# Weight sums of pair 0 made ahead for six feed-forward groups, four of them by way of DRAM

## The chip, the cores and the metric

The kernel runs on one core of one Trainium2 chip. The metric is the device time of one execution in microseconds (us), the median of several runs. The engines are named as in the profile: PE (TensorE, the matmuls), PEld (TensorE's weight loads), DVE (VectorE), ACT (ScalarE), POOL (GpSimd) and SP (SyncE, which here does nothing but issue DMAs). "SPq" is SP's queue of issues.

## The reference

One block of a network in float32, for 256 tokens of width 2048: a projection into several branches, a gated delta rule and a sparse attention, two gates, an output projection, and a feed-forward part with D_FF = 5632. The change bears on the feed-forward part's first matrix:

```python
x = layer_norm(DEEPNORM_ALPHA * x + merged @ w_out[l], ln1_g[l], ln1_b[l])
h_gate, h_up = jnp.split(x @ w_ffn_in[l], 2, axis=-1)
x = layer_norm(DEEPNORM_ALPHA * x + (jax.nn.silu(h_gate) * h_up) @ w_ffn_out[l], ln2_g[l], ln2_b[l])
```

## The kernel before

**Numbers in two parts.** PE multiplies in a short float type (`F32R`). Each float32 operand v is therefore split into a high part `hi` (a cast, on ACT) and a low part `lo = v - hi` (a subtraction, on DVE), and each product takes three matmuls: hi x hi, hi x lo, lo x hi (`mm3`, L213 to L215).

**Chunks.** Weights arrive as chunks of 128 x 1024 (512 KB). `chunk` (its DMA is L85, its cast L87, its subtraction L89) loads one into `raw` on SP and makes `hi` and `lo`. `raw`, `hi` and `lo` have four buffers each, so a load waits for a `raw` that ACT and DVE have done with, and a cast waits for a `hi` that PE has done with.

**Groups and pairs.** After the first layer norm the feed-forward part's first matrix is worked off in 512 gate and 512 up columns at a time: a first one in two blocks (`wfi`), then ten groups i = 1 to 10 (`wfg[i - 1]`, the loop from L1388 to L1399). A group has eight pairs q = 0 to 7, each of two chunks, and sums all of them in PSUM, for two blocks of 128 tokens and two halves of 512 columns. `x_group` (L1031) runs the pairs in a given order. A pair is done in one of two ways:

- plain (`plain_pair`): two chunks, eight products, 24 matmuls;
- with seven products (`seven_pair`, L265), after Strassen's way of multiplying 2 x 2 blocks: 21 matmuls. It needs differences of the activations (`f_form`, made once by `x_form`) and four sums of weight blocks, t1 to t4 (`sum13` L242, `sum24` L246 and L247), each split again (`f_thi` by ACT L237, `f_tlo` by DVE L238). Its loads are L276 (`f_wraw`) and L278 (`raw`). Where the sums are there already (`ready`), it loads one chunk and a half and makes none of them.

`FQ` lists the pairs with seven products: 4 and 6 in group 1, and 2, 4 and 6 in the others. The seven-product sums gather in four further PSUM banks; after the last such pair `sums_chain` (L1018) adds them up on DVE and ACT. The groups swap the two sets of four banks.

**After a group** `hidden_chain` (L1347) makes silu(gate) x up, transposes it on PE, splits it into the tiles `hH`, `hL` (from group 3 on at index i - 3), and makes forms of it for the second matrix. `hH7` to `hH10` hold the buffers of `seven_pair` until then (`f_home`: two each of `wraw`, `wt`, `thi`, `tlo`).

**What sets the order.** PE and SP run in the order in which the program is written; DVE, ACT and POOL are ordered by a scheduler, by priority:

```python
ctx.enter_context(tc.manual_schedule(engines={mybir.EngineType.PE, mybir.EngineType.SP}))
```

Work beside the matmuls is written as generators ("chains"). `tick()` is called after each chunk, or twice in a seven-product pair, and moves every chain on whose time has come; `yield n` waits n ticks, `yield "name"` for an event. `f_forms_chain` (L1330) makes the forms while the second `wfi` block and group 1 run. A DMA in a chain on SP takes its place in SP's order at the tick at which it is written.

Of the kernel before, what the change touches and what calls it, by code (L numbers as in the profile page):

```python
# [8 lines left out]
F32 = mybir.dt.float32  # L9
F32R = mybir.dt.float32r  # L10
# [7 lines left out]
P = 128  # L18
# [14 lines left out]
LEAD = 70  # L33
# [10 lines left out]
ZO = (0, 1, 3, 2, 4, 5, 6, 7)  # L44
OQ = (0, 2, 4, 6)
WALL = sorted({*WQ[0], *WQ[1]})
FQ = ((4, 6), *[(2, 4, 6)] * 9)
OUT_AT = (8, 9, 10)

LN2_LOAD = (5, 7, 9, 11)  # L50
# [9 lines left out]
def block_kernel(ctx: ExitStack, tc: tile.TileContext, xT, x, cpack, onehot, relb, convw, alog, dtb, gnw,  # L60
                 ws, wws, win, wz, wgt, wba, wbb, woa, wob, wfi, wfg, wfo, ln1g, ln1b, ln2g, ln2b, out):
    nc = tc.nc
# [6 lines left out]
    dr = ctx.enter_context(tc.tile_pool(name="dr", bufs=1, space=DRAM))  # L69
# [10 lines left out]
    def chunk(src, pool=None, lead=LEAD):  # L80
        n = src.shape[1]
        pool = pool or wp
        with tc.high_priority(offset=lead):
            raw = wp.tile([P, n], F32, name="raw", tag="raw")
            nc.sync.dma_start(raw, src)  # L85
            hi = pool.tile([P, n], F32R, name="hi", tag="hi")
            nc.scalar.copy(hi, raw)  # L87
            lo = pool.tile([P, n], F32R, name="lo", tag="lo")
            nc.vector.tensor_sub(lo, raw, hi.bitcast(F32))  # L89
        return hi, lo  # L90
# [5 lines left out]
    def start(gen, at_once=False):  # L96
        chains.append([gen, clock[0] + (next(gen) if at_once else 0)])
# [17 lines left out]
    def event(name):  # L115
        done[name] = clock[0]
# [86 lines left out]
    def split(hi, lo, src):  # L203
        nc.scalar.copy(hi, src)
        nc.vector.tensor_sub(lo, src, hi.bitcast(F32))
# [99 lines left out]
    def forms(g, a1, a2, b1, b2):  # L305

        nc.vector.tensor_sub(g[0], a2, b2)
        nc.vector.tensor_sub(g[1], a1, g[0])
        nc.vector.tensor_sub(g[2], a2, a1)
        nc.vector.tensor_sub(g[3], b1, g[1])  # L310
# [26 lines left out]
    def T(name, shape, dtype=F32, tag=None):  # L337
        return p1.tile(shape, dtype, name=name, tag=tag or name)
# [62 lines left out]
    def need(*names):  # L401
        for n in names:
            assert n in done, n
# [27 lines left out]
    for i in range(8):  # L431
        k0 = 2 * i
        parts = [srcs[i]] if i > 2 else [srcs[i][:, :512], srcs[i][:, 512:]]
        for j, src in enumerate(parts):
            k, n = k0 + j, 2 // len(parts)
# [8 lines left out]
            else:  # L444
                split(*xp, xr)
                hi, lo = chunk(src, lead=0)
# [28 lines left out]
    def taps(y, src, c):  # L475
        nc.scalar.activation(y, src, AF.Copy, scale=cw[:, c, 3:4])
        for j in (1, 2, 3):
            nc.vector.scalar_tensor_tensor(y[:, j:], src[:, :S - j], cw[:, c, 3 - j:4 - j], y[:, j:],
                                           op0=OP.mult, op1=OP.add)

    def conv_first(dst, pss):
        for i in range(4):
            taps(dst[:, i, :], pss[i // 2][:, (i % 2) * S:(i % 2 + 1) * S], 8 + i)
        nc.scalar.activation(dst[:, 0:4], dst[:, 0:4], AF.Silu)
# [436 lines left out]
    for ch in (gates_chain, key_chain, query_chain, value_chain, index_chain, attend_chain, out_gate_chain):  # L921
        start(ch())

    conv_first(s_kT, pss)
    event("kc0")
    for dst, h0, c0, ev in ((s_kT, 4, 12, "kc1"), (s_qT, 0, 0, "qc0"), (s_qT, 4, 4, "qc1"),
# [18 lines left out]
    def halves(*tiles):  # L945
        return [0, [t[:, i] for t in tiles for i in range(2)]]

    def two(name, dtype, old):
        return T(name, [P, 2, 1024], dtype, tag=old)

    def z_chain():

        yield "v1"
        yield 1
        t0 = [rp.tile([P, 2, 1024], F32R, name=f"z_t{i}", tag=f"x1_{i}") for i in range(2)]
        wt = two("z_wt", F32, "ol_")
        gates_home.update(wraw=halves(two("z_wraw", F32, "oh_")), wt=halves(wt), thi=halves(t0[0]), tlo=halves(t0[1]))
        for q, old in ((4, "s_ak"), (6, "s_sq")):
            t = T(f"g_form{q}", [P, 2, 4, P], F32R, tag=old)
            gates_form[q] = t[:, 0], t[:, 1]  # L960
        gates_form[2] = [p1.tile([P, 4, P], F32R, name="g_form2", tag="rel", bufs=2) for _ in range(2)]
        yield from early_sums(wz, ZQ[0], home, z_ready)
        yield 1
        x_form(ZQ[0], gates_form[ZQ[0]], wt[:, 0, :512], wt[:, 0, 512:])
        yield "lg"
        t1 = two("z_t2", F32R, "s_vT"), two("z_t3", F32R, "s_t")
        for tag, *t in zip(("thi", "tlo"), t0, t1):
            gates_home[tag] = halves(*t)
            gates_home[tag][0] = 2
        yield from early_sums(wz, ZQ[1], home, z_ready)  # L970
        for q in ZQ[1:]:
            yield 1
            x_form(q, gates_form[q], wt[:, 0, :512], wt[:, 0, 512:])
        event("zready")
# [35 lines left out]
    def x_form(q, dst, x32, g):  # L1010
        x32 = x32.rearrange("p (k t) -> p k t", k=2)
        g = g.rearrange("p (i t) -> p i t", i=4)
        ks = slice(2 * q % 4, 2 * q % 4 + 2)
        nc.vector.tensor_add(x32, XH[q // 2][:, ks].bitcast(F32), XL[q // 2][:, ks].bitcast(F32))
        forms([g[:, j] for j in range(4)], x32[:, 0, :P], x32[:, 0, P:], x32[:, 1, :P], x32[:, 1, P:])
        split(*dst, g)

    def sums_chain(v, wbank):  # L1018

        p1_, n6, n7, n5 = wbank  # L1020
        with tc.high_priority(offset=LEAD):
            nc.scalar.copy(v[0], p1_)
            nc.scalar.copy(v[2], n6)
            nc.vector.tensor_sub(v[2], v[2], p1_)
            nc.vector.tensor_add(v[1], n5, v[2])
        yield 1
        with tc.high_priority(offset=LEAD):
            nc.vector.tensor_add(v[2], v[2], n7)
            nc.vector.tensor_add(v[3], n5, v[2])

    def x_group(src, sevens, std, shared, form_of, home, sums, at={}, order=range(KT // 2), ready={}):  # L1031

        bank = [std() for _ in range(4)]
        sevens = [q for q in order if q in sevens]
        for q in order:
            if q in at:
                at[q]()
            if q in sevens:
                if q == sevens[0]:
                    wbank = [shared() for _ in range(4)]  # L1040
                seven_pair(bank, wbank, src, xh, xl, q, lambda q: lambda f: [t[:, f] for t in form_of[q]], home,
                           q == sevens[0], q == sevens[-1], ready)
                if q == sevens[-1]:
                    start(sums(wbank))
            else:
                plain_pair(bank, src, xh, xl, q, q == order[0], q == order[-1])
        return bank
# [129 lines left out]
    def load_x(tb, g):  # L1177
        if not g:
# [4 lines left out]
    bank = x_group(woa, OQ, ps_acc, ps_aux, gates_form, home,  # L1183
                   lambda wbank: seven_chain(0, wbank, wo_room[:, 1024:1536]), {q: lambda tb=tb: load_x(tb, 0) for tb, q in enumerate(OO[6:])}, OO,
                   wo_ready)
# [7 lines left out]
    hp_ = fh.enter_context(tc.tile_pool(name="hp", bufs=1, side="left", reuse_waits="tile"))  # L1193
    hH, hL = [None] * (FT // 4), [None] * (FT // 4)

    def h_tile(pool, i):
        hH[i], hL[i] = (pool.tile([P, 4, S], F32R, name=f"{hl}{i}", tag=f"{hl}{i}") for hl in ("hH", "hL"))
# [13 lines left out]
        nc.sync.dma_start(t.rearrange("p k t -> p (k t)").bitcast(F32), d_h[i, j])  # L1211

    h_first = passing()
    for i in range(1, 5):
        h_tile(hp_, i)
    l1 = ExitStack()
    gp = l1.enter_context(tc.tile_pool(name="gp1", bufs=1, side="left", reuse_waits="tile"))
    ex = l1.enter_context(tc.tile_pool(name="ex1", bufs=4, side="left", reuse_waits="tile"))
# [71 lines left out]
    def fv():  # L1290
        return fp.tile([P, 512], F32, name="v", tag="v", bufs=4)
# [20 lines left out]
                  lambda tb, ps: start(h_chain(0, tb, gated(tb, ps), ps_aux)))  # L1312
    l1.close()
    hp2 = fh.enter_context(tc.tile_pool(name="hp2", bufs=1, side="left", reuse_waits="tile"))
    for i in (5, 6):
        h_tile(hp2, i)


    f_home = {}
    for tag, dtype, i in (("wraw", F32, 7), ("wt", F32, 8), ("thi", F32R, 9), ("tlo", F32R, 10)):  # L1320
        f_home[tag] = [0, [hp2.tile([P, 1024], dtype, name=f"f_{tag}", tag=f"{hl}{i}") for hl in ("hH", "hL")]]

    def fhome(tag):
        e = f_home[tag]
        e[0] += 1
        return e[1][e[0] % 2]

    f_form = {}

    def f_forms_chain():  # L1330
        yield "x1"
        for tb in range(NTB):
            yield 2
            nc.sync.dma_start(d_x1[tb], x1[tb])
        t = [rp.tile([P, 2, 2, 4, P], F32R, name="f_form", tag=f"x1_{tb}") for tb in range(NTB)]
        for i, q in enumerate((4, 2, 6)):
            yield 1
            f_form[q] = t[i // 2][:, i % 2, 0], t[i // 2][:, i % 2, 1]
            x_form(q, f_form[q], fv(), fv())

    start(f_forms_chain())
    for tb, ps in enumerate(block_xs([wfi[1, k] for k in range(8)], xh, xl)):
# [45 lines left out]
    for i in range(1, NG + 1):  # L1388
        std, shared = (ps_aux, ps_acc) if i % 2 else (ps_acc, ps_aux)
        sums = []  # L1390

        def places():
            sums.extend(fv() for _ in range(4))
            return sums

        bank = x_group(wfg[i - 1], FQ[i - 1], std, shared, f_form, fhome, lambda wbank: sums_chain(places(), wbank))
        if i == NG:
            h_tile(hp2, 7)
        start(hidden_chain(i, bank, sums, std), at_once=True)  # L1399
# [58 lines left out]
    bank = group(0, ps_aux, ps_acc, FT // 2)  # L1458
# [4 lines left out]
    bank = group(1, ps_acc, ps_aux, FT // 2 - HELD)  # L1463
# [194 lines left out]
```

## Time and profile before

| | us |
|---|---|
| median of 3 runs (1456.36 to 1457.3) | 1456.81 |
| the profiled execution's own time | 1456.99 |
| its span, from the first to the last instruction | 1455.2 |
| PE busy, of the span | 1447.2 |
| DVE busy | 1253.8 |
| ACT busy | 807.3 |
| POOL busy | 47.6 |
| loads and stores over the span | 314.89 MB, mean 216 GB/s |

Busy PE is the time in which any matmul is under way; matmuls overlap, so it says only that PE waited little. The granted clock of PE was 0.999 over the span. In the rows a line starts with the time or the source line, then the engine, the operation, what it writes <- what it reads, and the shape.

### The profile page before, as it was taken

What the parts mean: (1) busy time and instruction counts of PE and PEld (TensorE: products, weight loads), DVE (VectorE), ACT (ScalarE), POOL (GpSimd) and SP (SyncE); (2) the same over time, 40 slices, a digit from 0 to 9 for tenths busy, and PEclk for the clock granted to TensorE, in tenths of its full rate; (3) what the DMA queues carried; (4) which work ended last, traced back from release to release, by engine and by line L of the source; (5) the groups of instructions that cost most, each with busy time, mean ns of one, the idle gap of its engine ahead of it and who ended that gap; (6) DMA issues with size and microseconds to landing.
All of it is one profiled execution on the core that took longest, in us unless ns stands there. A gap on an engine that the chain in (4) does not pass through costs nothing.

```text
span 1455.2 us, 19528 instructions
## 1 busy us (share of the span) xinstructions
PE 1447.2 (99%) x7158; PEld 1217.6 (84%) x7158; DVE 1253.8 (86%) x1713; ACT 807.3 (55%) x1000; POOL 47.6 (3%) x59
## 2 busy tenths in 40 slices
PE   9999999999999999999999999999999999999998
PEld 8888888888888888888888888888888888888887
DVE  6798985488699959998886899989999998989987
ACT  5765443457466646655445565656566565554552
POOL 0002010021000000000000000000000000000000
PEclk9999999999999999999999999999999999999999
DMA  8656575554556765765856667656666667887853
GB/s 290 196 160 196 174 187 167 170 165 152 173 198 221 234 201 201 239 187 198 314 191 226 223 241 243 208 204 210 224 206 213 215 217 247 311 341 264 325 206 117
DMA packets 95632, 314.89 MB, mean 216 GB/s; under 512 B 16992, under 2 KB 18184, under 8 KB 95024
## 3 DMA queue, kind: packets, MB, share of 16 engines
q1 hardware_dynamic: 84480, 296.93, 60.1%
q0 software_dynamic: 3872, 14.36, 3.1%
q10 hardware_dynamic: 7184, 2.36, 0.7%
q8 instruction: 56, 0.92, 0.3%
q14 instruction: 40, 0.33, 0.1%
HBM read 299.78 MB, written 13.83 MB: 216 GB/s over the span
## 4 chain that ended last, share of the span: by engine, by line
PE 98%; DMA 1%; DVE 0%; ACT 0%; issue 0%; POOLq 0%; SPq 0%; ACTq 0%
PE acc L214 11%; PE acc L215 11%; PE acc L213 11%; PE acc L149 10%; PE aux L215 10%; PE aux L214 10%; PE aux L213 10%; PE acc L152 5%; PE acc L171 4%; PE acc L169 4%; PE acc L170 3%; PE aux L171 1%; PE aux L170 1%; PE aux L169 1%; PE aux L733 1%; DMA raw<-in_win_dram 1%
## 5 line engine op out<-in xcount | busy, mean ns | idle before, releaser
L87 ACT CAST hi<-raw 128x1024 fp32r<-128x1024 f32 (+1 forms) x388 | 399.4, 1039 | 362.6 <-PE acc L149 87.5
L89 DVE TENSOR_TENSOR lo<-raw,hi 128x1024 fp32r<-128x1024 f32 (+1 forms) x388 | 466.6, 1213 | 121.8 <-ACT hi L87 118.9
L149 PE MATMUL acc<-X,hi 128*128 128x512 f32 x640 | 203.7, 400 | 0.0
L213 PE MATMUL acc<-hi,X 128*128 128x512 f32 x387 | 151.7, 392 | 0.0
L215 PE MATMUL acc<-hi,X 128*128 128x512 f32 x387 | 150.7, 389 | 0.0
L214 PE MATMUL acc<-lo,X 128*128 128x512 f32 x387 | 150.6, 389 | 0.0
L152 PEld LDWEIGHTS acc<-X,lo 128*128 128x128 f32 x640 | 120.2, 188 | 28.3
L213 PE MATMUL aux<-hi,X 128*128 128x512 f32 x331 | 129.4, 391 | 0.0
L215 PE MATMUL aux<-hi,X 128*128 128x512 f32 x331 | 128.9, 389 | 0.0
L214 PE MATMUL aux<-lo,X 128*128 128x512 f32 x331 | 128.8, 389 | 0.0
L152 PE MATMUL acc<-X,lo 128*128 128x256 f32 x640 | 126.0, 278 | 0.0
L149 PEld LDWEIGHTS acc<-X,hi 128*128 128x128 f32 x640 | 97.5, 189 | 2.0 <-ACT hi L87 0.7
L237 ACT CAST f_thi<-f_wt 128x1024 fp32r<-128x1024 f32 x58 | 61.1, 1054 | 52.5 <-DVE f_wt L247 30.9
L215 PEld LDWEIGHTS acc<-hi,X 128*128 128x128 f32 x387 | 72.6, 188 | 15.2
L213 PEld LDWEIGHTS acc<-hi,X 128*128 128x128 f32 x387 | 72.7, 188 | 14.9 <-ACT s_u L935 0.2
L214 PEld LDWEIGHTS acc<-lo,X 128*128 128x128 f32 x387 | 72.7, 188 | 14.7
L238 DVE TENSOR_TENSOR f_tlo<-f_wt,f_thi 128x1024 fp32r<-128x1024 f32 x58 | 70.0, 1219 | 6.3 <-ACT f_thi L237 6.0
L215 PEld LDWEIGHTS aux<-hi,X 128*128 128x128 f32 x331 | 62.1, 188 | 13.0
L214 PEld LDWEIGHTS aux<-lo,X 128*128 128x128 f32 x331 | 62.2, 188 | 12.8
L213 PEld LDWEIGHTS aux<-hi,X 128*128 128x128 f32 x331 | 62.1, 188 | 12.7
L237 ACT CAST thi<-wt 128x1024 fp32r<-128x1024 f32 x36 | 37.9, 1054 | 47.9 <-DVE wt L242 31.3
L169 PE MATMUL acc<-hi,X 128*128 128x512 f32 x160 | 64.3, 402 | 0.0
(619 smaller groups left out, 3012.9 us busy)
## 6 DMA issues: line engine op xcount, KB each, us to landing
raw<-in_wfg_dram SPq DMA_DIRECT2D x131, 512.0 KB, 4.2
raw<-in_wws_dram SPq DMA_DIRECT2D x80, 512.0 KB, 3.9
raw<-in_wfo_dram SPq DMA_DIRECT2D x70, 512.0 KB, 5.0
raw<-in_wgt_dram SPq DMA_DIRECT2D x49, 512.0 KB, 4.0
f_wraw<-in_wfg_dram SPq DMA_DIRECT2D x29, 512.0 KB, 6.0
raw<-in_win_dram SPq DMA_DIRECT2D x21, 512.0 KB, 3.7
wraw<-in_wfo_dram SPq DMA_DIRECT2D x18, 512.0 KB, 5.4
gt<-d_g SPq DMA_DIRECT2D x18, 512.0 KB, 6.8
```

What stands on the lines that cost most here:

```text
L87: nc.scalar.copy(hi, raw)
L89: nc.vector.tensor_sub(lo, raw, hi.bitcast(F32))
L149: nc.tensor.matmul(pss[c], hv[:, kk, cs[c]], X2[k // 4][:, k % 4], start=(k == 0), stop=False, skip_group_check=True)
L152: nc.tensor.matmul(pss[c][:, :S], lv[:, kk, cs[c]], xh[:, k, :], start=False, stop=(k == KT - 1), skip_group_check=True)
L169: nc.tensor.matmul(ps, xh, hv[:, kk], start=(k == 0), stop=False)
L170: nc.tensor.matmul(ps, xh, lv[:, kk], start=False, stop=False)
L171: nc.tensor.matmul(ps, xl, hv[:, kk], start=False, stop=(k == 2 * n - 1))
L213: nc.tensor.matmul(o, sh, hi, start=first, stop=False)
L214: nc.tensor.matmul(o, sh, lo, start=False, stop=False)
L215: nc.tensor.matmul(o, sl, hi, start=False, stop=last)
L237: nc.scalar.copy(hi, v)
L238: nc.vector.tensor_sub(lo, v, hi.bitcast(F32))
```

## The change

Pair 0 of groups 2 to 7 is done with seven products as well, and its four weight sums are made ahead, in place in the loaded chunks (`four_sums`):

- for groups 4 to 7 (`KEPT`) in the first stage of the kernel, from tick 56 on (`kept_chain`): loaded by SP, summed and split with low priority, and stored by POOL's queue into a DRAM tile `d_s`. They are loaded again by SP in `kept_load`, four DMAs of 512 KB, four ticks apart, begun in pair 4 of the group before, into the tiles of `hH5` and `hH6`, which each group's set uses in turn;
- for groups 2 and 3 (`NEAR`) at the end of `f_forms_chain`, into the tiles of `hH2` to `hH5`, where they stay until used. `hH1` takes the raw chunks.

These groups run their pairs in the order 1, 3, 2, 0, 4, 5, 6, 7 (`FO`). `thi` and `tlo` get a third buffer. The tiles `hH1` to `hH6` are taken up for their own purpose after groups 3 and 7. The forms are made in the order 4, 6, 2, 0.

```diff
-FQ = ((4, 6), *[(2, 4, 6)] * 9)
+KEPT = (4, 5, 6, 7)
+NEAR = (2, 3)
+FQ = ((4, 6), *[(0, 2, 4, 6) if i in KEPT + NEAR else (2, 4, 6) for i in range(2, 11)])
+FO = (1, 3, 2, 0, 4, 5, 6, 7)
+KEPT_FROM = 56
...
+    d_s = dr.tile([len(KEPT), 2, P, 2, 1024], F32, name="d_s")
+
+    def four_sums(ra, rb, lead=0):
+
+        r0, r1, s0, s1 = (t[:, n * 512:n * 512 + 512] for t in (ra, rb) for n in range(2))
+        with tc.high_priority(offset=lead):
+            nc.vector.tensor_add(r0, r0, s1)
+            nc.vector.tensor_add(s1, r1, s1)
+        yield 1
+        with tc.high_priority(offset=lead):
+            nc.vector.tensor_add(r1, r0, r1)
+            nc.vector.tensor_add(s0, r1, s0)
+
+    def kept_chain():
+        yield KEPT_FROM
+        raws = [T("k_raw", [P, 2, 1024], tag=t) for t in ("oh_", "s_x")]
+        hi = T("k_hi", [P, 2, 1024], F32R, tag="ol_")
+        for m, g in enumerate(KEPT):
+            raw = raws[m % 2]
+            for i in range(2):
+                nc.sync.dma_start(raw[:, i], wfg[g - 1, i])
+                yield 1
+            yield 1
+            for _ in four_sums(raw[:, 0], raw[:, 1], -LEAD):
+                yield 1
+            yield 1
+            for i in range(2):
+                with tc.high_priority(offset=-LEAD):
+                    for n in range(2):
+                        cs = slice(n * 512, n * 512 + 512)
+                        nc.scalar.copy(hi[:, i, cs], raw[:, i, cs])
+                        nc.vector.tensor_sub(raw[:, i, cs].bitcast(F32R), raw[:, i, cs], hi[:, i, cs].bitcast(F32))
+                yield 1
+                nc.gpsimd.dma_start(d_s[m, 0, :, i], hi[:, i].bitcast(F32))
+                nc.gpsimd.dma_start(d_s[m, 1, :, i], raw[:, i])
+        event("kept")
...
-    for i in range(1, 5):
-        h_tile(hp_, i)
+    near = [[hp_.tile([P, 1024], F32R if i > 1 else F32, name="near", tag=f"{hl}{i}") for hl in ("hH", "hL")]
+            for i in range(1, 5)]
...
-    for i in (5, 6):
-        h_tile(hp2, i)
+    near.append([hp2.tile([P, 1024], F32R, name="near", tag=f"{hl}5") for hl in ("hH", "hL")])
+    kept = [None, [hp2.tile([P, 1024], F32R, name="kept", tag=f"{hl}6") for hl in ("hH", "hL")]]
...
+    for tag in ("thi", "tlo"):
+        f_home[tag][1].append(hp2.tile([P, 1024], F32R, name="f_" + tag, tag=tag))
...
-        for i, q in enumerate((4, 2, 6)):
+        for i, q in enumerate((4, 6, 2, 0)):
             yield 1
             f_form[q] = t[i // 2][:, i % 2, 0], t[i // 2][:, i % 2, 1]
             x_form(q, f_form[q], fv(), fv())
+        yield 1
+        raw = near[0]
+        for m, g in enumerate(NEAR):
+            for i in range(2):
+                nc.sync.dma_start(raw[i], wfg[g - 1, i])
+                yield 1
+            yield 1
+            yield from four_sums(*raw)
+            for i in range(2):
+                yield 1
+                split(near[1 + 2 * m][i], near[2 + 2 * m][i], raw[i])
+            k_ready[g][0] = sums_of(near[1 + 2 * m], near[2 + 2 * m])
+            yield 4
...
+    def kept_load(m):
+
+        for i in range(2):
+            if m or not i:
+                kept[i] = [hp2.tile([P, 1024], F32R, name="kept", tag=f"{hl}{5 + i}") for hl in ("hH", "hL")]
+            for j in range(2):
+                if i or j:
+                    yield 4
+                nc.sync.dma_start(kept[i][j].bitcast(F32), d_s[m, j, :, i])
+        k_ready[KEPT[m]][0] = sums_of(*zip(*kept))
...
-        bank = x_group(wfg[i - 1], FQ[i - 1], std, shared, f_form, fhome, lambda wbank: sums_chain(places(), wbank))
+        at = {4: lambda: start(kept_load(KEPT.index(i + 1)))} if i + 1 in KEPT else {}
+        ready = k_ready.get(i)
+        if ready is not None:
+            at[0] = lambda ready=ready: ready[0]
+        bank = x_group(wfg[i - 1], FQ[i - 1], std, shared, f_form, fhome, lambda wbank: sums_chain(places(), wbank),
+                       at, range(8) if ready is None else FO, {} if ready is None else ready)
+        if i == NEAR[-1]:
+            for k in range(1, 5):
+                h_tile(hp_, k)
+        if i == KEPT[-1]:
+            for k in (5, 6):
+                h_tile(hp2, k)
```

More of the change, by code (lines that the diff above doesn't have):

```diff
@@ L922, in block_kernel @@
         start(ch())
+    d_s = dr.tile([len(KEPT), 2, P, 2, 1024], F32, name="d_s")
[31 more added lines that the diff above has]
+        event("kept")
+    start(kept_chain())
     conv_first(s_kT, pss)
@@ L954, in z_chain @@
         yield 1
+        need("kept")
         t0 = [rp.tile([P, 2, 1024], F32R, name=f"z_t{i}", tag=f"x1_{i}") for i in range(2)]
@@ L1325, in fhome @@
         e[0] += 1
-        return e[1][e[0] % 2]
+        return e[1][e[0] % len(e[1])]
     f_form = {}
@@ L1339, in f_forms_chain, with sums_of @@
             x_form(q, f_form[q], fv(), fv())
+        yield 1
[11 more added lines that the diff above has]
+            yield 4
+    k_ready = {g: {} for g in KEPT + NEAR}
+    def sums_of(hi, lo):
+        (t1, t2), (t4, t3) = ([(hi[i][:, n * 512:n * 512 + 512], lo[i][:, n * 512:n * 512 + 512]) for n in range(2)]
+                              for i in range(2))
+        return t1, t2, t3, t4
+    def kept_load(m):
[7 more added lines that the diff above has]
+        k_ready[KEPT[m]][0] = sums_of(*zip(*kept))
     start(f_forms_chain())
```

## The prediction

> **What bounds the kernel now.** I read the page first, then the busy time by stages, then the timelines of TensorE (PE) and of SyncE's queue (SP) around one feed-forward group.
>
> ```profile
> span 1455.2 us, 19528 instructions
> PE 1447.2 (99%) x7158; PEld 1217.6 (84%) x7158; DVE 1253.8 (86%) x1713; ACT 807.3 (55%) x1000; POOL 47.6 (3%) x59
> PE 98%; DMA 1%; DVE 0%; ACT 0%; issue 0%; POOLq 0%; SPq 0%; ACTq 0%
> ```
>
> The chain that ended last is PE for 98% of the span. A matmul taken away shortens the kernel, unless something makes PE wait that does not now. The stages show how near the next engine is; the rows are the weight part of groups 1, 2, 4 and 5 (a group runs from its pair 0 to the next group's pair 0):
>
> ```profile
> core 0: us, PE busy (x) PEld busy (x) DVE busy (x) ACT busy (x) POOL busy (x), PEclk, DMA share, GB/s
> 770.00:792.85 22.85, 22.85 (x103) 18.86 (x102) 16.57 (x25) 11.11 (x14) 0.00 (x0) 1.00 0.79 273
> 792.85:835.48 42.63, 42.63 (x191) 35.30 (x190) 33.81 (x42) 22.74 (x27) 1.11 (x2) 1.00 0.70 236
> 835.48:877.85 42.37, 42.37 (x192) 35.17 (x191) 40.98 (x49) 26.24 (x31) 2.12 (x4) 1.00 0.69 241
> 920.26:962.63 42.37, 42.37 (x192) 35.17 (x191) 38.40 (x44) 25.45 (x30) 0.00 (x0) 1.00 0.61 202
> 962.63:1005.04 42.41, 42.41 (x192) 35.18 (x191) 39.74 (x49) 25.85 (x31) 0.53 (x1) 1.00 0.61 207
> ```
>
> A group takes 42.4 us, PE never idles in it, and VectorE (DVE) is busy for 38 to 41 us of it. So DVE has only 1.4 to 4 us to spare in a group: it keeps up because it is fed far ahead. What PE spends on a pair:
>
> ```profile
> 979.20 0.39 PE L213 MATMUL aux<-hi,X 128*128 128x512 f32 x1
> ...
> 984.64 0.39 PE L213 MATMUL acc<-hi,X 128*128 128x512 f32 x1
> ...
> 989.40 0.39 PE L213 MATMUL aux<-hi,X 128*128 128x512 f32 x1
> ```
>
> Group 5's plain pair 3 starts at 979.20, its seven-product pair 4 at 984.64, its pair 5 at 989.40: 24 matmuls in 5.44 us and 21 in 4.76, 0.227 us each (the 0.39 is one's latency, they overlap).
>
> **The change, part by part.**
>
> *Fewer matmuls.* In groups 2 to 7 pair 0 becomes a seven-product pair: 24 - 21 = 3 matmuls less, six times: 18 x 0.227 = 4.1 us off PE, all of it on the path. At its own place the pair also costs DVE and ScalarE (ACT) less, since only a 1024 and a 512 wide chunk are split where two of 1024 were.
>
> ```profile
> L89 DVE TENSOR_TENSOR lo<-raw,hi 128x1024 fp32r<-128x1024 f32 x10 | 12.1, 1218 | 0.9 <-ACT hi L87 0.8
> L246 DVE TENSOR_TENSOR f_wt<-f_wt,f_wraw 128x512 f32<-128x512 f32 x3 | 2.0, 682 | 0.0
> L307 DVE TENSOR_TENSOR fg<-v 128x128 f32<-128x128 f32 x1 | 0.3, 281 | 0.0
> ```
>
> That is 1.22 - 0.68 = 0.54 us of DVE per group, so DVE's 39.7 becomes about 39.2 against 41.7 on PE.
>
> *Sums made early for groups 4 to 7.* Per group four adds and four subtracts of 512 at 0.68 are 5.4 us of DVE, 22 us for four, with 16 casts of 512 on ACT, 8 loads on SP and 16 stores on GpSimd's queue. They come from tick 57 of the first stage on (about 211 us on PE; SP reaches them some 20 us sooner) and last 28 ticks of 2.8 us:
>
> ```profile
> 216.00:252.00 36.00, 36.00 (x270) 31.54 (x268) 22.27 (x42) 13.56 (x18) 0.00 (x0) 1.00 0.58 172
> 252.00:288.00 36.00, 36.00 (x239) 31.50 (x237) 18.62 (x24) 13.92 (x20) 0.00 (x0) 1.00 0.47 149
> ```
>
> In 72 us DVE idles 31, GpSimd does nothing at all and the DMA engines are half busy: the cover is there, I take 0. The third load waits on SP for the first store, with chunk loads queued behind it, but it comes 7 ticks (20 us) after that store is written down, as long as SP's lead. Below 0 nothing can come of added work. Without the cover each of the 32 DVE operations could hold a step of the inversion by 0.7 us; that a few of them do is worth up to 3 us.
>
> *Sums made in place for groups 2 and 3, and one more set of forms.* 2 x (4 x 0.68 + 2 x 1.22) = 10.3 us of DVE and 2.5 us for the forms of pair 0 (two operations of 0.68, four of 0.28): 12.8 us, spread from 770 us into group 2, where the rows leave 6.3 + 8.8 + 1.4 = 16.5 us. Cost 0; if the second set falls wholly into group 2 (40.98 - 0.54 + 5.2 = 45.6 us of DVE against 41.7 of PE) up to 3.9 us. The second set's loads wait on SP for DVE to finish the first set, 10 ticks after its loads; chunk loads stand behind them for a few us of a lead of 17. 0.
>
> *The reload: 16 DMAs on SP, and a wait.* In groups 3 to 6 the first reload DMA is issued inside pair 4, just behind pair 4's own two loads. It writes into the tile that pair 0 of the same group reads, and in the new order (1, 3, 2, 0, 4, 5, 6, 7) pair 0 stands right before pair 4. So SP must wait until PE is three matmuls from the end of pair 0, and pair 5's chunks are queued behind. Where SP stands now at that place:
>
> ```profile
> 963.02 0.42 SPq L276 DMA_DIRECT2D f_wraw<-in_wfg_dram  x1
> 965.22 0.33 SPq L278 DMA_DIRECT2D raw<-in_wfg_dram  x1
> 972.28 1.43 SPq L85 DMA_DIRECT2D raw<-in_wfg_dram  x2
> 973.76 0.42 SPq L276 DMA_DIRECT2D f_wraw<-in_wfg_dram  x1
> ```
>
> Pair 4's loads go out at 963.02 and 965.22, pair 5's at 972.28; PE ends the pair before pair 4 at 984.64. SP is 12 us early, and the wait takes all of it away: pair 5's chunks would leave no longer 17 us but 5 us ahead of PE. That SP really stands still at such a wait, with the loads behind it, is seen where it waits for VectorE in the layer norm:
>
> ```profile
> 754.71 0.42 SPq L1334 DMA_DIRECT2D d_x<-x  x1
> 769.31 0.33 SPq L85 DMA_DIRECT2D raw<-in_wfi_dram  x1
> ```
>
> For 14.6 us no load left. The Trainium skill, "DMA: Bandwidth & Descriptors", section "Anatomy of one DMA", says why: DMA engines do not wait on semaphores, the issuing sequencer does before dispatch. By that rule the free reload below (1452.7) is excluded; by the rows alone it keeps a small chance.
>
> What it takes from issue to a usable chunk, from the chain of waits at the start:
>
> ```profile
> 22.53 4.65 DMA raw<-in_win_dram
> 27.27 1.05 ACT hi L87
> 28.35 1.24 DVE lo L89
> ```
>
> And how DMAs queued together land, three issues of 512 KB on SP's timeline and then the landing of each:
>
> ```profile
> 1284.86 0.33 SPq L85 DMA_DIRECT2D raw<-in_wfo_dram  x1
> 1285.24 0.42 SPq L1441 DMA_DIRECT2D x<-d_x  x1
> 1285.72 0.42 SPq L276 DMA_DIRECT2D wraw<-in_wfo_dram  x1
> DMA to landing us min/median/max: 3.5/3.5/3.5
> DMA to landing us min/median/max: 4.8/4.8/4.8
> DMA to landing us min/median/max: 5.7/5.7/5.7
> ```
>
> They land at 1288.3, 1290.0 and 1291.4: 3.5 us for the first, about 1.35 more (1.7 at most) for each behind it. Let T be the moment that PE frees the tile. The reload leaves at T and lands at T+3.5; pair 5's first chunk leaves at T+0.4 and lands at T+4.8; cast, T+5.85; difference, T+7.1. PE has three matmuls and pair 4 left, and reaches pair 5 at T+5.3: it waits 0.6 us for the cast (first matmul) and 1.0 us for the difference (second matmul), 1.6 us. Then pair 5's second chunk and pair 6's two loads land at T+6.2, 7.5 and 8.9, and DVE, idle from T+1.4 to T+5.9 with nothing loaded, has its sums for pair 6 to do without a lead. I laid the group out step by step in this way (PE and SP in the order written, ACT and DVE taking the earliest-written operation that is ready, durations from the rows): pair 6's last low part is ready at T+16.3 where PE is there at T+15.9, 0.4 us; the last sum of the seven-product banks ends at T+23.65 where the next group's first matmul, which takes over those banks, is due at T+22.9, 0.8 us. In all 2.7 us for each reload, so the group takes 44.4 us where without the wait it would take 41.7. The same laying out gives the kernel before 42.4 us a group and no wait, as the rows have it. Bounds: 0 if the wait is covered after all; 5.5 if DVE's fixed order puts pair 5's first difference ahead of pair 4's last low part: that is then ready at T+8.3 instead of T+3.9, 4.4 us late, and the 1.2 us behind it stay. I take 2.7, as both engines' rows lead to it. The other three reload DMAs of a group find their tile free and cost SP 0.4 us each.
>
> By the skill's fit on the same page and section (2.0 us plus bytes at 436 GB/s) a load of 512 KB takes 3.2 us and the one behind it 1.2 more, so pair 5's chunk would be there 0.4 us sooner and the sum would come out 1.6 us lower, an estimate of 1462.1; the trace's 3.5 stands.
>
> *Sum.* -4.1 + 4 x 2.7 = +6.9 us (2.74 unrounded) on the profiled execution of 1456.99 (span 1455.2 and 1.8 around it), which stands 0.2 above the median of 1456.81: 1463.7 as a median.
>
> **The rivals.** 0.2% of this kernel, 2.9 us, is about what can be told from no change.
>
> 1. *The wait costs nothing* (the other side): pair 5 is covered by something that the rows don't show, and only the matmuls count: 1456.8 - 4.1 = 1452.7. For it: DVE is ahead of PE now, and SP was seen standing for 14.6 us without PE waiting. Against it: there the chunks still left 12 us ahead of PE; here 5 us are left, and issue to difference alone took 7.1 us at the start of the kernel. It decides below 0.3 us a reload.
> 2. *The wait is smaller than the chain says*, 0.3 to 1.75 us a reload, as it would be if PE waited only for pair 5's first chunk and all later lateness were absorbed: 4 x 1.0 - 4.1 = 0, within 0.2%, 1456.8.
> 3. *DVE's order makes it worse*: 4 x 5.5 - 4.1 = +18, 1475. For it: in group 5 one chunk's difference (972.13) ran ahead of the second low part of the pair before it (974.40). Against it: pair 4's own low parts ran ahead of pair 5's chunk there.
> 4. *The early sums hold up the first stage*: +1 to +3 on top of any case; in the range, no case of its own.
>
> **How the numbers follow.** Forecast, reloads at 1.75 to 4 us each, 1459.7 to 1469: 0.56. Rival 1: 0.14. Rival 2: 0.16. Rival 3: 0.14. Faster is rival 1, same is rival 2, slower the forecast and rival 3, 0.70. The range takes in rival 1 and the forecast with the first stage's 2 us, 1452.4 to 1471, and leaves out rival 3; the forecast's own range is 1459.7 to 1469.
>
> **What would show it.** 7140 matmuls. On SP's timeline a gap before the first reload of each of groups 3 to 6, ended by PE near the end of pair 0, and pair 5's loads 0.4 us behind it. Windows of these reload cycles (from one pair 5 to the next) at 44.4 us with PE waits of 0.6 and 1.0 us on the cast and difference of pair 5; group 2 and the groups' cycles without a reload wait at 41.7 or 42.4. From 216 to 288 us DVE some 20 us busier and PE still at 36.00 in each slice. The forecast is wrong if pair 5's loads leave before pair 0 ends, or if they leave late and PE does not wait.

## The result and the profile after

The changed kernel takes 1474.63 us (median of 4 runs, 1474.15 to 1477.47) beside 1456.59 us for the kernel before on the same chip: a ratio of 1.0125, 95% interval 1.0112 to 1.0137. That is slower, as forecast, but 10.9 us above the forecast of 1463.7 and outside its range. The profiled execution took 1474.24 us. Its page, with the span, the busy times and the chain that ended last:

```profile
span 1472.5 us, 19637 instructions
PE 1452.1 (99%) x7140; PEld 1216.0 (83%) x7140; DVE 1278.7 (87%) x1763; ACT 815.6 (55%) x1021; POOL 56.2 (4%) x75
PE 66%; DVE 5%; DMA 3%; issue 1%; ACT 1%; SPq 0%; POOLq 0%; ACTq 0%; DVEq 0%
```

The 18 matmuls are gone (7158 to 7140), yet the chain is no longer PE alone: DVE, DMA and ACT are on it. (Its shares add up to 76% because it could be followed back only to 360 us; the 66% is therefore not to be set beside the 98% of before.) The waits view says for what PE waited (total us, times, longest; `acc` and `aux` are the two sets of PSUM banks):

```profile
PE acc L217 <- ACT hi L91: 3.4, 2, 2.0
PE aux L217 <- ACT hi L91: 3.2, 2, 1.8
PE aux L218 <- DVE lo L93: 1.5, 2, 0.8
PE acc L218 <- DVE lo L93: 1.5, 2, 0.8
...
PE acc L218 <- DVE f_tlo L242: 0.8, 1, 0.8
PE aux L218 <- DVE f_tlo L242: 0.8, 1, 0.8
...
PE acc L217 <- DVE v L1072: 0.4, 1, 0.4
```

Four waits on a cast (up to 2.0 us) and four on the difference behind it: the first two matmuls of pair 5 in groups 3 to 6. Two more, on `f_tlo`, stand in pair 6. (Lines 217 to 219 were 213 to 215 before.) SP's timeline at the second of the four reloads:

```profile
946.85 0.33 SPq L1415 DMA_DIRECT2D kept<-d_s  x1
947.34 0.80 SPq L89 DMA_DIRECT2D raw<-in_wfg_dram  x2
948.20 0.42 SPq L280 DMA_DIRECT2D f_wraw<-in_wfg_dram  x1
948.71 0.48 SPq L282 DMA_DIRECT2D raw<-in_wfg_dram  x1
949.25 0.49 SPq L1415 DMA_DIRECT2D kept<-d_s  x1
949.90 0.39 SPq L89 DMA_DIRECT2D raw<-in_wfg_dram  x1
```

and PE's timeline there, from pair 0's last matmuls to pair 5's first (the bracket is the idle time before, and what ended it):

```profile
946.65 0.39 PE L217 MATMUL acc<-kept,X 128*128 128x512 f32 x1
...
951.87 0.39 PE L219 MATMUL acc<-f_thi,X 128*128 128x512 f32 x1
953.65 0.50 PE L217 MATMUL acc<-hi,X 128*128 128x512 f32 x1 [1.39 <-ACT hi L91]
954.91 0.76 PE L218 MATMUL acc<-lo,X 128*128 128x512 f32 x1 [0.76 <-DVE lo L93]
955.47 0.63 PE L219 MATMUL acc<-hi,X 128*128 128x512 f32 x1
955.89 0.63 PE L217 MATMUL acc<-hi,X 128*128 128x512 f32 x1
...
958.43 0.40 PE L217 MATMUL acc<-hi,X 128*128 128x512 f32 x1
```

PE reads the tile until it starts pair 0's last three matmuls at 946.65; SP lets the reload go at 946.85 = T, and pair 5's two chunks, pair 6's loads and the next reload follow within 3 us. Without the wait PE would have started pair 5 at 952.10 (T+5.25, forecast T+5.3). It starts at 953.65, loses 1.03 more before its second matmul (954.91 - 953.65 - 0.23), and then something unplanned: matmuls 0.43 us apart instead of 0.227. The windows view has it, with PE's granted clock in the column behind POOL:

```profile
core 0: us, PE busy (x) PEld busy (x) DVE busy (x) ACT busy (x) POOL busy (x), PEclk, DMA share, GB/s
903.78:907.19 3.41, 1.93 (x9) 1.23 (x7) 0.29 (x1) 1.04 (x1) 0.00 (x0) 1.00 0.98 334
...
951.57:954.98 3.41, 1.26 (x6) 0.48 (x4) 1.26 (x2) 2.09 (x2) 0.00 (x0) 1.00 1.02 418
954.98:958.39 3.41, 3.41 (x8) 2.70 (x9) 3.36 (x3) 1.67 (x2) 0.00 (x0) 0.50 1.03 419
...
999.35:1002.77 3.42, 1.73 (x6) 1.22 (x7) 1.68 (x2) 1.92 (x2) 0.00 (x0) 1.00 0.99 395
1002.77:1006.18 3.41, 3.41 (x9) 2.65 (x9) 2.29 (x3) 1.66 (x2) 0.00 (x0) 0.50 1.03 422
...
1043.72:1047.14 3.42, 1.60 (x8) 0.98 (x6) 0.00 (x0) 0.91 (x1) 0.00 (x0) 1.00 0.96 339
```

After two of the four waits (the second and the third) PE ran for 3.41 us at half clock: eight or nine matmuls where 15 fit, about 1.6 us lost each time. After the first and the fourth, with no less idle time in all, it did not. The two slow stretches begin 47.79 us apart, which is 14 times 3.41; the other rows are laid on the same steps of 3.41 us, the one at each wait in which PE did least.

To see where the time went, both profiled executions are set side by side at the same marks (the end of each group's transposes). The changed kernel is 1.4 us behind before group 1, 2.0 after it, 1.3 after group 2, 18.2 after group 6 and 17.5 after group 7, where it stays. So group 2 and group 7 each save 0.7 as forecast, the first part loses 1.4, group 1 loses 0.7, and the four reload cycles lose 16.9, of which 8.2 was forecast (4 x (2.74 - 0.68)). With the 0.68 that each cycle saves in matmuls put back, PE waits or runs slowly for 5.1, 4.6, 5.0 and 4.9 us in the four cycles (at pair 5, at half clock, at pair 6, once at the next bank), where 2.7 was forecast.

### The profile page after: what moved, and what is told of

It reads as the page before. It is cut to its first block, busy times and chain, and to the rows that moved or that the text cites. A ratio compares the mean times of both kernels' runs of the same rounds, so it can differ in the third digit from the quotient of the medians.

```text
span 1472.5 us, 19637 instructions
## 1 busy us (share of the span) xinstructions
PE 1452.1 (99%) x7140; PEld 1216.0 (83%) x7140; DVE 1278.7 (87%) x1763; ACT 815.6 (55%) x1021; POOL 56.2 (4%) x75
## 4 chain that ended last, share of the span: by engine, by line
PE 66%; DVE 5%; DMA 3%; issue 1%; ACT 1%; SPq 0%; POOLq 0%; ACTq 0%; DVEq 0%
PE acc L218 9%; PE acc L219 9%; PE acc L217 9%; PE aux L218 8%; PE aux L219 8%; PE aux L217 8%; PE acc L175 2%; PE acc L173 2%; PE acc L174 2%; DMA f_wraw<-in_wfg_dram 2%; PE aux L175 1%; PE aux L173 1%; PE aux L174 1%; DVE lo L93 1%; DVE lo L242 1%
## 5 line engine op out<-in xcount | busy, mean ns | idle before, releaser
L217 PE MATMUL acc<-hi,X 128*128 128x512 f32 x369 | 145.7, 395 | 4.3 <-ACT hi L91 3.4
L218 PE MATMUL acc<-lo,X 128*128 128x512 f32 x369 | 144.6, 392 | 1.5 <-DVE lo L93 1.5
L219 PE MATMUL acc<-hi,X 128*128 128x512 f32 x369 | 144.4, 391 | 0.0
L217 PE MATMUL aux<-hi,X 128*128 128x512 f32 x313 | 123.3, 394 | 3.2 <-ACT hi L91 3.2
L218 PE MATMUL aux<-lo,X 128*128 128x512 f32 x313 | 122.7, 392 | 1.5 <-DVE lo L93 1.5
L219 PE MATMUL aux<-hi,X 128*128 128x512 f32 x313 | 122.4, 391 | 0.0
L217 PEld LDWEIGHTS acc<-hi,X 128*128 128x128 f32 x369 | 69.7, 189 | 20.0 <-ACT hi L91 4.2
L218 PEld LDWEIGHTS acc<-lo,X 128*128 128x128 f32 x369 | 69.7, 189 | 16.3 <-DVE lo L93 2.1
L219 PEld LDWEIGHTS acc<-hi,X 128*128 128x128 f32 x369 | 69.7, 189 | 14.6
L217 PEld LDWEIGHTS aux<-hi,X 128*128 128x128 f32 x313 | 59.1, 189 | 16.1 <-ACT hi L91 4.1
L218 PEld LDWEIGHTS aux<-lo,X 128*128 128x128 f32 x313 | 59.2, 189 | 14.3 <-DVE lo L93 2.1
L219 PEld LDWEIGHTS aux<-hi,X 128*128 128x128 f32 x313 | 59.2, 189 | 12.4
L173 PE MATMUL acc<-hi,X 128*128 128x512 f32 x160 | 64.3, 402 | 0.0
```

Source lines behind the costliest of these rows:

```text
L173: nc.tensor.matmul(ps, xh, hv[:, kk], start=(k == 0), stop=False)
L217: nc.tensor.matmul(o, sh, hi, start=first, stop=False)
L218: nc.tensor.matmul(o, sh, lo, start=False, stop=False)
L219: nc.tensor.matmul(o, sl, hi, start=False, stop=last)
```

## The experiments

The expectations below use these theories. **W**: SP stands at the reload until PE frees the tile, pair 5's loads stand behind it, and that is the whole loss. **S**: the added work itself (the sums, their splits, the third buffers) costs the time on DVE. **Q**: the 16 reload DMAs cost it by their traffic, wherever they wait. **L**: the reload lands late because of the way the DRAM tile is laid out. All edits are made to the changed kernel. Every run is set against runs of the kernel before on its own chip (medians 1456.58 to 1456.78).

### The reload on another queue

```diff
-                nc.sync.dma_start(kept[i][j].bitcast(F32), d_s[m, j, :, i])
+                nc.gpsimd.dma_start(kept[i][j].bitcast(F32), d_s[m, j, :, i])
```

> The changed kernel with its 16 reload DMAs issued by GpSimd's queue instead of SyncE's; nothing else differs. Theory W (SyncE stands still at the first reload of each of groups 3 to 6 with pair 5's loads behind it, and this costs about 19.6 us in all): the four waits and the slow stretches behind them go, SyncE is again some 12 us ahead at pair 5, the four cycles fall from 46.6 us to 41.7, and the time is 1474.6 - 19.6 = 1455.0. Rival S (the added sums, stores and 21 MB of traffic slow the kernel, whoever issues them): the time stays over 1470.

Measured: 1455.48, ratio 0.9988 (0.9979 to 0.9997). The same bytes into the same tiles, with the same wait for PE, but no weight load queued behind it. In the groups PE waits neither for `hi` nor for `lo` any more; of the waits on weights one is left, in group 7:

```profile
PE acc L218 <- DVE f_tlo L242: 0.8, 1, 0.8
```

19 us come back by moving the wait. S and Q fall as causes of it: the added work and the traffic are all still there.

### The reload later, in the group that uses it

```diff
-                    yield 4
+                    yield 1
...
-        at = {4: lambda: start(kept_load(KEPT.index(i + 1)))} if i + 1 in KEPT else {}
+        at = {FO[0]: lambda: start(kept_load(KEPT.index(i)))} if i in KEPT else {}
```

> The changed kernel with the reload still on SyncE in program order, but begun in pair 1 of the group that uses it, one tick apart, 20 us after the tile is free. W: SyncE, 17 us ahead of PE there, finds the tile free and stands nowhere; 1455.0 as with GpSimd's queue, within 1 us. Rival S: over 1470. Rival Q (it is not the wait but 16 more loads of 512 KB in SyncE's queue, which hold up the chunks behind them): now four of them come within 8 chunks instead of spread over seven pairs, so PE waits at pairs 3, 2 and 0, and the time stays over 1465.

Measured: 1454.72, ratio 0.9986 (0.9977 to 0.9995). The reload stays on SP, four pairs later in its order, and when its turn comes the tile has been free for 7 to 9 us (20 were expected).

### Only the early sums

The first stage makes and stores the sums; no pair uses them, nothing is reloaded, and groups 2 and 3 get none either.

```diff
-FQ = ((4, 6), *[(0, 2, 4, 6) if i in KEPT + NEAR else (2, 4, 6) for i in range(2, 11)])
+FQ = ((4, 6), *[(2, 4, 6)] * 9)
...
-        at = {4: lambda: start(kept_load(KEPT.index(i + 1)))} if i + 1 in KEPT else {}
-        ready = k_ready.get(i)
+        at = {}
+        ready = None
```

> The sums of groups 4 to 7 are made and stored in the first stage, but no group uses any: pairs, order and forms of the groups are those of before, no sums for groups 2 and 3, no reload. It measures the first stage alone. From the trace of the changed kernel (its marks are 1.3 us late when the merged gates are transposed, at 631 us): W: 1456.6 + 1.3 = 1457.9. Rival S: the first stage carries a large part, 1462 or more. As predicted (nothing): 1456.6.

Measured: 1457.93, ratio 1.0011 (1.0002 to 1.0019): the early sums cost 1.2 us (0.3 to 2.8). The prediction had put 0, with a bound of 3. In the changed kernel the stage looks so:

```profile
216.00:252.00 36.00, 36.00 (x267) 31.52 (x266) 30.20 (x55) 15.68 (x23) 4.33 (x8) 1.00 0.96 322
252.00:288.00 36.00, 35.73 (x239) 31.12 (x237) 28.55 (x40) 19.23 (x29) 4.25 (x8) 1.00 0.81 291
```

DVE is 17.9 us busier than before (58.75 against 40.88), and still PE idles only 0.27 us here. The DMA engines go from 0.58 and 0.47 to 0.96 and 0.81. In this run by itself PE's longest wait in the stage, at 255 us, is:

```profile
PE aux L617 <- ACT s_t L623: 1.0, 1, 1.0
```

A wait on `s_t` there (0.3 to 1.1 us) is in nine of the ten profiled executions that make the early sums, and in neither of the two that don't. In this run PE falls 1.2 us behind the kernel before at that wait.

### Only groups 2 and 3

```diff
-FQ = ((4, 6), *[(0, 2, 4, 6) if i in KEPT + NEAR else (2, 4, 6) for i in range(2, 11)])
+FQ = ((4, 6), *[(0, 2, 4, 6) if i in NEAR else (2, 4, 6) for i in range(2, 11)])
...
-    start(kept_chain())
...
-        ready = k_ready.get(i)
+        ready = k_ready.get(i) if i in NEAR else None
```

> Only the sums of groups 2 and 3 are made ahead and used (nothing in the first stage, no DRAM, no reload); groups 4 to 10 as before. Two pairs with three matmuls less are 1.4 us; the trace of the changed kernel shows a wait of 0.5 us at the end of group 1. W: 1456.6 - 1.4 + 0.5 = 1455.7. Rival S: DVE, with 10 us of work more in groups 1 and 2, makes PE wait, 1459 or more.

Measured: 1455.58, ratio 0.9991 (0.9982 to 1.0): 1.15 us less for six matmuls, which are worth 1.36. By the medians the sums made in place are close to free, as the prediction had it, though in the profiled execution PE waits 0.6 us on `v` at the end of group 1.

### The DRAM tile in one piece for each reload

```diff
-    d_s = dr.tile([len(KEPT), 2, P, 2, 1024], F32, name="d_s")
+    d_s = dr.tile([len(KEPT), 2, 2, P, 1024], F32, name="d_s")
...
-                nc.sync.dma_start(kept[i][j].bitcast(F32), d_s[m, j, :, i])
+                nc.sync.dma_start(kept[i][j].bitcast(F32), d_s[m, j, i])
```

(and the same in the two stores). In the change each reload gathers 128 rows of 4 KB that lie 8 KB apart; here they lie back to back.

> The changed kernel with the DRAM tile laid out so that each reload of 512 KB is one piece (before, rows of 4 KB at a stride of 8 KB); the wait on SyncE stays. In the changed kernel the first reload lands 4.2 to 4.4 us after its issue and pair 5's first chunk 5.6 to 6.3 us after it, where the prediction had 3.5 and 4.8. Theory L (the stride makes the reload slow): 3.5 and 4.8, each of the four waits of PE at pair 5 falls by 0.8 to 1.2 us, and fewer stretches at half clock: 1474.6 - 5 = about 1469 to 1470. Rival M (any DMA that reads this much lands so in a burst, whatever its rows): no change, 1474.6 within 1 us.

Measured: 1468.62, ratio 1.0076 (1.0063 to 1.0089), 6.0 us less than the change. Issue to landing of the first reload of a set and of the first chunk queued behind it, in the changed kernel:

```profile
DMA to landing us min/median/max: 4.4/4.4/4.4
DMA to landing us min/median/max: 5.5/5.5/5.5
```

and here:

```profile
DMA to landing us min/median/max: 3.6/3.6/3.6
DMA to landing us min/median/max: 4.5/4.5/4.5
```

3.6 and 4.5 are the prediction's figures (3.5 and 4.4 from issue), 4.4 and 5.5 are not. PE's waits follow:

```profile
PE acc L218 <- DVE lo L93: 1.5, 2, 0.8
PE aux L218 <- DVE lo L93: 1.5, 2, 0.8
PE acc L218 <- DVE f_tlo L242: 1.4, 2, 0.8
PE acc L217 <- ACT hi L91: 1.4, 2, 0.7
PE aux L217 <- ACT hi L91: 1.2, 2, 0.7
```

0.5 to 0.7 for the cast where the change has 1.4 to 2.0, so that pair 5 costs 1.7 to 1.9 us (from the starts) where 1.6 was forecast. L is right: the layout accounts for a third of the loss against the kernel before, and for more than half of the miss. No window of the groups runs at half clock any more: after the same wait PE does 17 matmuls in 3.3 us.

```profile
951.70:955.00 3.30, 1.87 (x7) 1.17 (x7) 2.36 (x2) 2.81 (x3) 0.00 (x0) 1.00 1.02 418
955.00:958.30 3.30, 3.30 (x17) 2.69 (x15) 3.24 (x5) 1.49 (x3) 0.00 (x0) 1.00 1.03 416
```

### Six idle matmuls ahead of pair 5

To tell what the half clock is worth, groups 3 to 6 multiply by a tile of zeros six times ahead of pair 5 (which adds nothing to the sums), 1.4 us that PE would otherwise spend waiting.

```diff
+            for _ in range(fill if q == 5 else 0):
+                nc.tensor.matmul(bank[0], zero, X2[0][:, 0], start=False, stop=False, skip_group_check=True)
```

> The changed kernel with six matmuls of 128x512 more ahead of pair 5 in groups 3 to 6, with a weight tile of zeros that adds nothing, in PE's order where it stands waiting (6 x 0.227 = 1.36 us each, less than the shortest wait for pair 5's cast, 1.56). In the trace of the changed kernel two of the four waits are followed by 3.3 us at a granted clock near 0.5 (0.52 in one window). Theory C (PE's clock is halved because PE stood idle for most of some 3.3 us; busy PE keeps it): no window near half, 1474.6 - 3.4 = about 1471. Rival: the clock has nothing to do with the wait, the fill lies within it, and the time is 1474.6; or the fill only adds, 1474.6 + up to 5.4.

Measured: 1473.61, ratio 1.0111 (1.0097 to 1.0125), which overlaps that of the change. The half clock is gone in the profile:

```profile
951.00:954.50 3.50, 3.30 (x16) 2.41 (x14) 0.06 (x1) 1.05 (x1) 0.00 (x0) 1.00 1.01 401
954.50:957.90 3.40, 2.64 (x11) 1.95 (x12) 3.25 (x3) 2.72 (x3) 0.00 (x0) 1.00 1.02 418
957.90:961.30 3.40, 3.40 (x17) 2.81 (x16) 3.40 (x5) 1.87 (x2) 0.00 (x0) 1.00 0.97 386
```

but in the third cycle, where the change had lost 1.6 us at half clock and 0.2 at pair 6, PE now waits 1.7 us at pair 6. DVE is what is late there, and a slow PE had let it catch up. By the marks the second cycle adds 2.4 us to the lag behind the kernel before, where it added 3.9 in the change; the other three cycles add what they did, within 0.1. So where PE is kept busy the half clock does not come, and in these two executions it cost about 1.5 us in one cycle and nothing in the other. The medians differ by 1.0 us, too little to confirm that.

### A tile of its own for every second reload

```diff
-                kept[i] = [hp2.tile([P, 1024], F32R, name="kept", tag=f"{hl}{5 + i}") for hl in ("hH", "hL")]
+                kept[i] = [hp2.tile([P, 1024], F32R, name="kept", tag=f"{hl}{5 + i}" if i or m % 2 else f"{hl}own") for hl in ("hH", "hL")]
```

(the third buffers of `thi` and `tlo` make room for it).

> The changed kernel with its reload on SyncE at the same place and pace, but every second group's first reload tile is another one, so that the tile written is never the one that pair 0 of the running group reads; for room the third buffers of the split sums (thi, tlo) are taken out again. W (what costs is that the tile is still in use): SyncE stands nowhere, 1455.0. If the reloads' place in SyncE's order or the burst of loads costs by itself: over 1465. If the third buffers matter, some us over 1455.

Measured: 1454.60, ratio 0.9985 (0.9976 to 0.9994). The reload stands at the change's place in SP's order, on SP, and no longer waits. It goes out 17 us ahead of the time at which the change lets it go, with pair 5's loads on their old lead:

```profile
882.01 0.33 SPq L282 DMA_DIRECT2D raw<-in_wfg_dram  x1
882.39 0.42 SPq L1413 DMA_DIRECT2D kept<-d_s  x1
889.07 1.43 SPq L89 DMA_DIRECT2D raw<-in_wfg_dram  x2
```

From group 2 on PE saves 0.7 us in each group to 7, by the marks. This is the direct test of W: same queue, same place, same bytes, no wait, 20 us less.

### The reload one pair later

```diff
-                    yield 4
+                    yield 3
...
-        at = {4: lambda: start(kept_load(KEPT.index(i + 1)))} if i + 1 in KEPT else {}
+        at = {5: lambda: start(kept_load(KEPT.index(i + 1)))} if i + 1 in KEPT else {}
```

> The changed kernel with the reload begun one pair later, in pair 5 (three ticks apart instead of four): pair 5's two loads leave ahead of the wait, pair 6's stand behind it. SyncE is still some 12 us early and waits, but PE then has pairs 4 and 5 to do: 5.3 + 5.4 = 10.7 us of cover instead of 5.3. Pair 6's first load lands about 6 us after the wait ends, its second 7.5, its sums are split 7 to 9 us after that. W with the wait's price set by the cover: PE waits 0 to 1.5 us at pair 6, and the time is 1455 to 1461. Rival (a standing SyncE costs the same wherever it stands): 1474.

Measured: 1457.83, ratio 1.0011 (1.0002 to 1.002). Now pair 5's loads stand ahead of the reload and pair 6's behind it. Only pair 6 waits:

```profile
PE acc L218 <- DVE f_tlo L242: 1.3, 2, 0.7
...
PE aux L218 <- DVE f_tlo L242: 0.5, 1, 0.5
```

One pair more of lead turns some 5 us a cycle into 0.3 to 1.0: the loss goes by how near to its use the load behind the wait is.

### Both at once, and the last wait of group 1

Two attempts at more: the tile of its own together with the one-piece layout (the two diffs above), and the tile of its own with the sums of groups 2 and 3 at low priority.

> The reload into a tile of its own (as in e7_own) and the DRAM tile laid out so that each reload is one contiguous piece (as in e5_flat), together. If the strided rows cost time only by way of the wait on SP, nothing waits any more and the layout is worth nothing here: 1454.6, as e7_own, within 0.7. If the strided stores or loads cost time by themselves (the stores in the first stage, where 1.2 us were lost, or the reloads' share of the DMA engines), up to 1.2 us less: 1453.4.

Measured: 1454.95, ratio 0.9987 (0.9978 to 0.9996). The layout is worth nothing once nothing waits for the landing.

```diff
-            yield from four_sums(*raw)
+            yield from four_sums(*raw, -LEAD)
...
-                split(near[1 + 2 * m][i], near[2 + 2 * m][i], raw[i])
+                with tc.high_priority(offset=-LEAD):
+                    split(near[1 + 2 * m][i], near[2 + 2 * m][i], raw[i])
```

> e7_own, and the sums made in place for groups 2 and 3 get low priority on DVE and ACT (an offset of -70, as the early sums have). If these sums are what PE's wait of 0.7 to 0.9 us in group 1 comes from (on v, line 1072, at about 838 us), it goes and the time is 1453.8; if that wait comes from DVE being full there in any order, it stays, 1454.6; if the low priority puts the sums of group 3 behind that group's first need, PE waits there for f_thi or f_tlo in its pair 0 and the time is above 1456.

Measured: 1455.53 (1452.57 to 1459.43), ratio 0.9997 (0.9988 to 1.0006). In the profile the wait on `v` in group 1 is gone, and that execution took 1452.57, but it was the quickest of 11; the median is no better. Nor does one profile without the wait show that these sums bring it on: of the nine profiled executions that make them at full priority seven have the wait and two don't (one pair later, and both at once), and the two without these sums (before, and only the early sums) don't have it either. To give way to everything makes the time uneven, and from one profile I can't say where the other runs lose.

## Why the prediction was wrong

- **Right**: the matmuls (7140; 0.7 us saved in groups 2 and 7, and in groups 2 to 7 once nothing waits); the place of the wait, SP's standstill until PE frees the tile with pair 5's loads 0.4 to 0.5 us behind; PE's arrival at pair 5 (T+5.3, measured T+5.25); the two steps of the wait, cast and then difference. The Trainium skill's rule cited there ("DMA: Bandwidth & Descriptors", section "Anatomy of one DMA"), that the issuing sequencer does the waiting before dispatch, agrees with all four reloads: nothing behind them left SP before they did, and a wait on another queue, or none, gave back 19 to 20 us.
- **The step that failed: the landing.** "The reload leaves at T and lands at T+3.5; pair 5's first chunk leaves at T+0.4 and lands at T+4.8": these were read from loads that are one piece in DRAM. The reload's rows of 4 KB lie 8 KB apart. It landed after 4.2 to 4.4 us, and pair 5's first chunk at T+5.6 to T+6.3. PE lost 2.6 to 3.2 us at pair 5 instead of 1.6. With the one-piece layout the reload lands after 3.6 to 3.7, the chunk at T+4.9 to T+5.0, the wait is 1.7 to 1.9, and 6.0 of the 10.9 us come back. (The chunk was put 1.3 us behind the reload where the row that it was read from has 1.7; in the one-piece run 1.3 is what came, so that choice was not the error.) The Trainium skill's fit (same page and section), which the prediction set aside, gives 3.2, an estimate that would have missed by more; the section is on DMAs that GpSimd issues, and these are SP's.
- **Pair 6 was sized too low, again by the landings.** Forecast 0.4; where PE runs at full clock, in the first and the last cycle, it is 1.4. Its sums wait for loads of which the last lands at T+9.5 to T+11.6 (forecast T+8.9). In the one-piece run it lands at T+8.7 in the second cycle, and there PE does not wait; in the other three it lands at T+10.5 to T+10.8, and PE waits 1.3, 0.8 and 1.5. One thing that sets these three apart is a store of 512 KB that GpSimd issues 2.3 to 2.8 us behind the reload and that the second cycle doesn't have:

```profile
903.23 0.53 POOL L1462 DMA_DIRECT2D d_g<-gs  x1 [6.87 <-DVE gs L209]
993.50 0.53 POOL L1462 DMA_DIRECT2D d_g<-gs  x1 [89.74 <-DVE gs L209]
1037.75 0.53 POOL L1462 DMA_DIRECT2D d_g<-gs  x1 [43.72 <-DVE gs L209]
```

The changed kernel shows the same split (T+11.4 to T+11.6 with the store, T+9.5 without). The prediction's landings took no account of it. That it is what delays the loads is argued from these cycles alone; no run moves the store. The 0.8 us at the next bank, on the other hand, was 0.4 once and otherwise not seen.

- **The half clock was not in the sum.** Two stretches, some 1.6 us of PE each. The Trainium skill, "TensorE: Matmul & The Clock Gate", section "Part 1: The HAM clock gate", has PE fall to half clock after an idle window of about 3.4 us, in windows whose beginning does not depend on the kernel. The trace agrees in the length of the slow stretches (3.41 us) and in their distance, a whole number of such windows. It differs in that PE was not wholly idle in the window ahead (1.26 and 1.73 us busy), so less than an idle window is enough. By the run with the idle matmuls a stretch can add its 1.5 us to the total or nothing.
- **Two covers were thinner than stated.** The first stage's 0 was 1.2 (within its bound of 3), and group 1 lost 0.7 where 0 was put (0 to 2.2 in the other runs that make the same sums).
- **Rivals.** That the wait costs nothing (1452.7) and that it is smaller (1456.8) are out. The third gave 1475, and the time is near it by luck, for its mechanism is not what happened: it had PE wait in pair 4 for a low part, and the timeline shows pair 4 running through to 951.87 without a gap.

In the sum of the profiled executions: the reload cycles lost 16.9 where 8.2 was forecast, the stages before them 2.0 where 0 was, the other two groups saved 1.4 as forecast; 17.5 against 6.9.

## What to carry to other kernels

A DMA that must wait for a tile should not stand in a queue ahead of loads with less lead than its wait: here four such DMAs cost 20 us, and another queue, a tile that is free, or a place four pairs later each gave it back. When a wait eats up the lead, every microsecond of landing counts on the path, so take a landing time from a transfer of the same layout, not just of the same size, and ask what else is under way at the time. And the gain of the idea itself, 4.1 us of matmuls, shrank to about 2 even at its best, because the work it added before was not quite free: with a tile of its own the marks lose 1.6 us up to the end of group 1 and gain 4.1 behind it.

## What the runs showed of the hardware that was not expected

- A load of 512 KB as 128 rows of 4 KB, 8 KB apart in DRAM, landed 0.6 to 0.8 us later than in one piece (4.2 to 4.4 us against 3.6 to 3.7, four reloads each), and the load queued behind it 0.7 to 1.3 us later from its issue (5.1 to 5.8 against 4.4 to 4.5). Whether all of that is the read or also where the rows lie in DRAM, no run here tells.
- PE dropped to half clock for 3.41 us after steps of 3.41 us in which it was busy for 1.26 and 1.73 us, and not after steps with 1.93 and 1.60. The last is less than 1.73, so the busy time in a step, as the profile has it, does not by itself tell where the line lies. The idle time of the first and the fourth wait was about as long, but spread over two steps.
